# Memory attention by query rows, and a dilated layer whose keys and queries are made with tokens on the partitions

## The chip, the cores and the metric

The kernel runs on one core of a Trainium2 chip. The metric is device time in microseconds of one execution. TensorE (PE) multiplies, VectorE (DVE), ScalarE (ACT) and GpSimd (POOL) do the rest, SyncE (SP) issues the transfers. Engines run side by side, each through its own queue in order, and wait for each other through semaphores.

## What is computed

A network for 512 tokens of 1024 features: a first block (three kinds of attention, gates, a feed-forward part) and a second one (an mLSTM layer, a dilated-window layer, and a gated addition `ple` behind each). The two parts that the change touches:

```python
def memory_attention(cq, mk, mv):          # 4 heads of 128, 256 memory rows
    logits = jnp.einsum('bshd,bmhd->bhsm', cq, mk).astype(jnp.float32) * C_HEAD_DIM ** -0.5
    p = jax.nn.softmax(logits, axis=-1).astype(mv.dtype)
    return jnp.einsum('bhsm,bmhd->bshd', p, mv).reshape(bsz, seq, C_DIM)

def shared_kv(h, norm_g, w_kv, knorm_g, cos, sin):
    kv = (rms_norm(h, norm_g) @ w_kv).astype(jnp.float32)
    k, v = jnp.split(kv, 2, axis=-1)       # 4 heads of 128 each
    k = apply_rope(rms_norm(k, knorm_g), cos, sin)
    return k, v

def dilated_layer(h, k, v, norm_g, w_in, qnorm_g, w_out, cos, sin):
    proj = rms_norm(h, norm_g) @ w_in
    q, z = jnp.split(proj, [B_QW], axis=-1)            # 3 groups x 4 heads x 128, and 512
    q = apply_rope(rms_norm(q, qnorm_g), cos, sin)
    # group 0: window 128, step 1; group 1: window 512, step 4; group 2: window 2048, step 16
    # softmax of each group, the groups weighted by their log-denominators
    y = o.reshape(Bsz, S, B_VW) * jax.nn.silu(z.astype(jnp.float32))
    return y.astype(h.dtype) @ w_out
```

`rms_norm` is taken over the 1024 features of `h` (with gain `norm_kv` for K and V, `norm_b` for the rest) and again over the 128 features of each head of K and Q (gains `knorm`, `qnorm_b`).

## The kernel before

Activations lie feature-major: a tile of 128 features by 512 tokens, eight of them for 1024 features. A product in near-float32 is three fp32r matmuls of the operands' high and low halves (`mm3`: hi·hi, hi·lo, lo·hi). Weights come in units of 128 x 1024 float32 through SyncE's queue into `wraw` (two buffers); ScalarE rounds a unit to its high half `wh` (L154), and the low half `wl` is a subtraction on GpSimd (L158) or VectorE (L160), as the counter `pool_share` says (0.5: every second unit on GpSimd; 1.0: all; 0: none). A unit holds the eight 128 x 128 blocks of one output tile (24 matmuls of 512 columns), and a generator `fm_g` yields in the middle, so that "half a tile" is 12 matmuls. TensorE runs its instructions as they are coded; on the other engines a scheduler sets the order.

Memory attention (L655 to L715) weaves its steps with 20 half tiles of other products (queries of heads 2 and 3, and the gates): `logits(h)` makes memory rows by queries in two PSUM banks `zps`, copies them (L669), takes the maximum of both (L671) and over the partitions by an all-reduce on GpSimd (L673), subtracts it (L675) and takes the exponent; `values(h)` multiplies with `mv`, sums the columns by two matmuls with a matrix of ones (`colsum`), and divides through Ln and Exp, with `y` at L695. Behind it comes the stick-breaking attention, and the top-k search of the first attention runs on VectorE beside both.

The dilated layer makes each head's K and Q as a feature-major tile and calls `rope` on it: times the token's rms factor `bc` (L1370), squares in two halves `sqh`, `sql` (L1374 to L1376), the rotation (L1380 to L1383, two of its operations on GpSimd), and later, out of the list `todo`, the column sum over the head's 128 features, Ln, Exp and the product `q`, `kT`, `kTp` (L1391, L1394). 16 tiles go through it. The input's halves `xs` are split twice (`xsplit`, L241 and L242), once scaled by `norm_kv` and once by `norm_b`. `main` weaves `logits` and `values` of the four heads with the making of the other heads' Q and z; `logits(h)` ends with masks, a maximum, an all-reduce (L1500), subtractions and exponents; `values(h)` ends with `y` at L1539. Then `finish(h)` multiplies by silu(z) and splits, `out` and `prods` are the output product.

Of the kernel before, what the change touches and what calls it, by code (L numbers as in the profile page):

```python
# [47 lines left out]
def constants():  # L48
# [11 lines left out]
    cos, sin = np.cos(ang).T, np.sin(ang).T  # L60
    cos2 = np.concatenate([cos, cos], 0)
    sin2 = np.concatenate([sin, -sin], 0)
# [26 lines left out]
class K:  # L89
# [46 lines left out]
    def pre(s, *spec):  # L136
# [9 lines left out]
        if u == 0:  # L146
            for c in (slice(0, 512), slice(512, 1024)):
                s.split(hi[:, c], lo[:, c], raw[:, c])
            s.ready[spec] = hi, lo
            return  # L150
# [395 lines left out]
    def dsa_mem(s, x, iqc):  # L546
# [5 lines left out]
        with ExitStack() as br:  # L552
# [101 lines left out]
            with ExitStack() as c:  # L654
# [4 lines left out]
                zps = s.pool("zps", 2, PSUM, ctx=c)  # L659
# [4 lines left out]
                def logits(h):  # L664
                    z = wk.tile([128, 2, T], F32, name="z")
# [4 lines left out]
                    mx = s.tmp.tile([128, T], F32, name="t512")  # L670
                    nc.vector.tensor_tensor(mx, z[:, 0], z[:, 1], op=OP.max)  # L671
                    mb = wk.tile([128, T], F32, name="mb")
# [4 lines left out]
                    es = wk.tile([128, T], F32, name="es")  # L677
                    nc.gpsimd.tensor_tensor(es, z[:, 0], z[:, 1], op=OP.add)
                    e = [w1.tile([128, 2, T], F32R, name="e%d" % i) for i in range(2)]
                    s.split(e[0], e[1], z)  # L680
                    S = [w1.tile([128, T], F32R, name="S%d" % i) for i in range(2)]
                    s.split(S[0], S[1], es)
                    st[h] = e, S

                def values(h):
                    e, S = st.pop(h)
                    op = ops.tile([128, T], F32, name="ops")
                    for m in range(2):
                        s.mm3(op, [x[:, m, 128 * h:128 * h + 128] for x in mv], [x[:, m] for x in e], m == 0, m == 1)
                    dp = s.colsum(S[0], S[1], ops)  # L690
# [5 lines left out]
                    if s.dbg: s.dbg("attC%d" % h, y)  # L696
# [1002 lines left out]
```

## Time and profile before

| | |
|---|---|
| Time, median of 3 runs | 1631.87 us (1630.12 to 1631.94) |
| Profiled execution | 1637.18 us |
| Its span, first to last instruction | 1635.4 us |
| Granted TensorE clock, mean | 0.968 |
| Busy: PE, DVE, ACT, POOL | 1519.9, 1032.5, 704.3, 446.0 us |

The profile shows one execution. A busy share is the time in which an engine has an instruction in work; the matmuls' ends are modelled and overlap the next one's start, so their pace is read from starts. An idle time is put down to the instruction whose end released the engine.

### The profile page before, as it was taken

What the parts mean: (1) busy time and instruction counts of PE and PEld (TensorE: products, weight loads), DVE (VectorE), ACT (ScalarE), POOL (GpSimd) and SP (SyncE); (2) the same over time, 40 slices, a digit from 0 to 9 for tenths busy, and PEclk for the clock granted to TensorE, in tenths of its full rate; (3) what the DMA queues carried; (4) which work ended last, traced back from release to release, by engine and by line L of the source; (5) the groups of instructions that cost most, each with busy time, mean ns of one, the idle gap of its engine ahead of it and who ended that gap; (6) DMA issues with size and microseconds to landing.
All of it is one profiled execution on the core that took longest, in us unless ns stands there. A gap on an engine that the chain in (4) does not pass through costs nothing.

```text
span 1635.4 us, 17606 instructions
## 1 busy us (share of the span) xinstructions
PE 1519.9 (93%) x6717; PEld 1226.6 (75%) x6725; DVE 1032.5 (63%) x1313; ACT 704.3 (43%) x1019; POOL 446.0 (27%) x244
## 2 busy tenths in 40 slices
PE   8988998999999999999999998999999998867788
PEld 5866777777778887888888886778778786655677
DVE  7876878864766737433243337844576479878766
ACT  5633335454445545322232325343654365333553
POOL 3323432222311403110011105310120026865432
PEclk9998999999999999999999999999999999878999
DMA  5311322123222433332333333223212332311132
GB/s 192 115 52 52 93 76 77 52 65 103 84 80 82 136 116 127 98 103 91 99 95 100 94 97 122 78 78 117 65 52 78 132 108 64 102 52 39 39 123 97
DMA packets 44917, 148.11 MB, mean 91 GB/s; under 512 B 5280, under 2 KB 6688, under 8 KB 44576
## 3 DMA queue, kind: packets, MB, share of 16 engines
q1 hardware_dynamic: 44832, 146.98, 28.3%
q8 instruction: 53, 0.87, 0.2%
q14 instruction: 32, 0.26, 0.1%
HBM read 139.60 MB, written 6.29 MB: 89 GB/s over the span
## 4 chain that ended last, share of the span: by engine, by line
PE 56%; DVE 18%; ACT 7%; issue 6%; POOL 4%; DMA 2%; SPq 0%; POOLq 0%; DVEq 0%; ACTq 0%
PE dps L128 41%; PE b L128 10%; PE z L128 3%; POOL wl L158 1%; DVE e L808 1%; ACT e L122 1%; DVE e L809 1%; ACT t L122 1%; DVE sql L1376 1%; DVE t L1381 1%; PE aps L128 1%; DVE ss L290 1%; PE o L128 1%; DVE xl L242 1%; DVE t L1382 1%
## 5 line engine op out<-in xcount | busy, mean ns | idle before, releaser
L128 PE MATMUL dps<-xh,wl 128*128 128x512 f32 (+2 forms) x1092 | 430.3, 394 | 16.6 <-POOL wl L158 16.6
L128 PE MATMUL dps<-xh,wh 128*128 128x512 f32 (+2 forms) x1092 | 435.6, 399 | 7.0 <-DVE aTl L239 5.8
L128 PE MATMUL dps<-xl,wh 128*128 128x512 f32 (+2 forms) x1092 | 429.5, 393 | 4.5 <-DVE xl L242 4.5
L154 ACT ACTIVATE wh<-wraw 128x1024 fp32r<-128x1024 f32 x213 | 225.1, 1057 | 452.3 <-PE dps L128 280.6
L158 POOL TENSOR_TENSOR wl<-wraw,wh 128x1024 fp32r<-128x1024 f32 x88 | 224.0, 2546 | 535.3 <-ACT wh L154 351.5
L160 DVE TENSOR_TENSOR wl<-wraw,wh 128x1024 fp32r<-128x1024 f32 x151 | 191.2, 1267 | 170.1 <-ACT wh L154 169.5
L128 PEld LDWEIGHTS dps<-xh,wl 128*128 128x128 f32 (+1 forms) x1092 | 207.7, 190 | 62.3 <-POOL wl L158 17.8
L128 PEld LDWEIGHTS dps<-xh,wh 128*128 128x128 f32 (+1 forms) x1092 | 207.9, 190 | 57.4 <-DVE aTl L239 7.5
L128 PEld LDWEIGHTS dps<-xl,wh 128*128 128x128 f32 (+1 forms) x1092 | 207.8, 190 | 49.8 <-DVE xl L242 5.5
L1025 POOL TENSOR_TENSOR g<-g,bc 128x512 f32<-128x512 f32 x22 | 38.9, 1769 | 245.7 <-ACT g L122 245.7
L128 PE MATMUL b<-xl,wh 128*128 128x512 f32 x224 | 90.9, 406 | 8.1 <-DVE xl L242 8.0
L128 PE MATMUL b<-xh,wh 128*128 128x512 f32 x224 | 91.9, 410 | 3.0 <-ACT xh L241 1.6
L128 PE MATMUL b<-xh,wl 128*128 128x512 f32 x224 | 90.5, 404 | 4.0 <-DVE wl L160 3.9
L128 PE MATMUL dps<-fh,wh 128*128 128x512 f32 x176 | 69.3, 394 | 0.0
L128 PE MATMUL dps<-fh,wl 128*128 128x512 f32 x176 | 69.0, 392 | 0.0
L128 PE MATMUL dps<-fl,wh 128*128 128x512 f32 x176 | 68.3, 388 | 0.0
L128 PE MATMUL b<-wh,xh 128*128 128x512 f32 x160 | 63.5, 397 | 3.2 <-DVE y L695 2.2
L242 DVE SCALAR_TENSOR_TENSOR xl<-h,vecs,xh 128x512 fp32r<-128x512 f32 x56 | 60.3, 1092 | 6.8 <-ACT xh L241 6.7
L128 PE MATMUL b<-wl,xh 128*128 128x512 f32 x160 | 62.9, 393 | 0.8 <-DVE wl L160 0.8
L128 PE MATMUL b<-wh,xl 128*128 128x512 f32 x160 | 63.0, 394 | 0.0
L128 PEld LDWEIGHTS b<-xl,wh 128*128 128x128 f32 x224 | 43.5, 194 | 21.3 <-DVE xl L242 11.4
L1034 DVE TENSOR_TENSOR f<-dps,g 128x512 f32<-128x512 f32 x20 | 13.8, 692 | 67.3 <-PE dps L128 64.4
(366 smaller groups left out, 2676.9 us busy)
## 6 DMA issues: line engine op xcount, KB each, us to landing
wraw<-in_W SPq DMA_DIRECT2D x239, 512.0 KB, 3.6
h<-in_x SPq DMA_DIRECT2D x16, 256.0 KB, 4.0
pw<-pwo SPq DMA_DIRECT2D x16, 256.0 KB, 2.5
pw<-pw SPq DMA_DIRECT2D x2, 2048.0 KB, 7.8
strip<-in_relb SPq DMA_DIRECT2D x8, 256.0 KB, 2.7
out<-h SPq DMA_DIRECT2D x7, 256.0 KB, 2.0
G<-in_mem SPq DMA_DIRECT2D x1, 1024.0 KB, 9.0
praw<-in_p SPq DMA_DIRECT2D x2, 512.0 KB, 3.9
```

The lines of the kernel that those rows point to most:

```text
L122: i = s.nc.scalar.activation(out, in_, func, **kw)
L128: s.nc.tensor.matmul(out, l, r, start=start, stop=stop, skip_group_check=True)
L154: nc.scalar.activation(hi, raw, AF.Copy)
L158: nc.gpsimd.tensor_tensor(lo, raw, hi.bitcast(F32), op=OP.subtract)
L160: nc.vector.tensor_tensor(lo, raw, hi.bitcast(F32), op=OP.subtract)
L242: nc.vector.scalar_tensor_tensor(lo, src, scale, hi.bitcast(F32), op0=OP.mult, op1=OP.subtract)
L290: nc.vector.tensor_tensor(S[0], S[0], t, op=OP.add)
L808: nc.vector.tensor_tensor_scan(e[:, ::-1], keep, e[:, ::-1], 0.0, op0=OP.mult, op1=OP.add)
L809: nc.vector.tensor_tensor(c, c, e, op=OP.subtract)
L1025: nc.gpsimd.tensor_tensor(g, g, st["bc"], op=OP.mult)
L1376: nc.vector.tensor_tensor(sql, sq, sqh.bitcast(F32), op=OP.subtract)
L1381: nc.vector.tensor_tensor(t2[0:64], x[64:128], cs[64:128, T:], op=OP.mult)
```

## The change

Memory attention makes its logits the other way round: 128 query rows by 256 memory rows, four of them in the two banks `z`. The maximum and the sum are then along the row (a reduction on VectorE, an accumulator of ScalarE's exponent), the division is a multiply per row, and the result is transposed back by eight 128 x 128 transposes a head (`transp`) ahead of `values`. The all-reduce, the sum `es` and the column sums are gone.

The dilated layer makes K, Q (three groups of four tiles) and V in a new way, `quad`: the fixed side of the matmul is 128 tokens of `xs` (for K and Q every fourth token, so that a tile holds one class modulo 4), the moving side the weights of four tiles, 512 columns. `rope` then works on 128 tokens by four tiles: squares summed along the row by ScalarE's accumulator, the rotation wholly on VectorE, the factors as small 128 x 16 operations. `turned` transposes back to feature-major tiles, out of which `keys` and `queries` copy; they are called as hooks in the middle of the next group's product. The gains `norm_kv` and `norm_b` are multiplied into the weights as they are split (`quad` units in two pieces of 512 columns, `fmg` units in eight of 128), so that `xs` is split once, unscaled, where the `ple` before makes it; `knorm` and `qnorm_b` go into the tables of cosines by two multiplies at the start. `pool_share` is 0, and the additions of `logits` move to VectorE. The column sum in `values` becomes one float32 product with ones. The written order of the layer is new too; the host gives the tables with tokens on the partitions.

```diff
 def logits(h):                               # memory attention
-    for m in range(2):
-        zp = zps.tile([128, T], F32, name="zps")
-        s.mm3(zp, [k[:, h, 128 * m:128 * m + 128] for k in mk], cq[h], True, True)
-        nc.scalar.activation(z[:, m], zp, AF.Copy)
-    nc.vector.tensor_tensor(mx, z[:, 0], z[:, 1], op=OP.max)
-    nc.gpsimd.partition_all_reduce(mb, mx, 128, RMAX)
-    for m in range(2):
-        nc.vector.tensor_tensor(z[:, m], z[:, m], mb, op=OP.subtract)
-    s.act(z, z, AF.Exp, scale=sc)
-    nc.gpsimd.tensor_tensor(es, z[:, 0], z[:, 1], op=OP.add)
+    for t in range(4):
+        s.mm3(zt[:, t], [q[:, qt] for q in cq[h]], [k[:, h] for k in mk], t % 2 == 0, True)
+    nc.vector.tensor_reduce(mx, zt, mybir.AxisListType.X, OP.max)
+    nc.vector.tensor_scalar(nm, mx, -sc, None, op0=OP.mult)
+    for t in range(4):
+        s.act(e[:, t], zt[:, t], AF.Exp, scale=sc, bias=nm[:, t:t + 1], accum_out=sm[:, t:t + 1])
+    nc.vector.reciprocal(rs, sm)
+    for t in range(4):
+        nc.vector.tensor_scalar(e[:, t], e[:, t], rs[:, t:t + 1], None, op0=OP.mult)
 def main():
     for h in range(4):
         logits(h)
-        yield 4 if h else 3
+        yield 2 if h else 3
         if h:
+            transp(h - 1)
+            yield 2
             values(h - 1)
-    yield 4
+    yield 2
+    transp(3)
+    yield 2
     values(3)
     yield 1
...
+def quad(wname, c0s, gain, hooks, classes=True):
+    pss = [s.b4.tile([128, T], F32, name="b4") for _ in range(4)]
+    for k in range(8):
+        if k % 2 == 0:
+            u = s.w("quad", wname, tuple(c0s), k // 2, gain)
+        c = slice(512 * (k % 2), 512 * (k % 2) + 512)
+        for t in range(4):
+            r = slice(t, T, 4) if classes else slice(128 * t, 128 * t + 128)
+            s.mm3(pss[t], (xs[0][:, k, r], xs[1][:, k, r]), (u[0][:, c], u[1][:, c]), k == 0, k == 7)
+        for f in hooks.get(k, ()):
+            f()
+    return pss
...
+r = rstd_g()
+pk = quad("w_kv_2", [128 * h for h in range(4)], "norm_kv", {2: [lambda: next(r)], 4: [lambda: next(r)]})
+XK = rope(pk, ck)
+X0 = qquad(0, {5: [keys]})
+X1 = qquad(1, {5: [lambda: queries(X0, QS[0])]})
+logits(0)
+z_tile(0)
+pv = quad("w_kv_2", [512 + 128 * h for h in range(4)], "norm_kv", {5: [lambda: queries(X1, QS[1])]}, False)
...
+logits(1)
+z_tile(1)
+X2 = qquad(2, {4: [lambda: values(0)]})
+z_tile(2)
+values(1)
+z_tile(3)
+for h in range(2):
+    finish(h)
+queries(X2, QS[2])
+logits(2)
+out = s.fm4_g("w_out_b_2", [128 * m for m in range(4)], xs, ev, ks=range(4))
+prods(4, range(2))
+logits(3)
+next(out)
+next(out)
+values(2)
+finish(2)
+next(out)
+values(3)
+finish(3)
```

Where memory attention's head 2 begins, TensorE had before (`e`, `S` of the head before, `ops` a PSUM bank, `mk` and `cq` of head 2):

```order
L128 MATMUL ops<-e_964,mv_194 128x512
L128 MATMUL ops<-e_965,mv_194 128x512
L128 MATMUL ops<-e_964,mv_195 128x512
L128 MATMUL ops<-S_968,onesr 128x512
L128 MATMUL ops<-S_969,onesr 128x512
L128 MATMUL zps<-cq_934,mk_192 128x512
L128 MATMUL zps<-cq_935,mk_192 128x512
L128 MATMUL zps<-cq_934,mk_193 128x512
```

Of the change, the same engine at the transposes of head 1 (`ops<-csts,e`; the `dps` rows are the other products):

```order
L128 MATMUL dps<-xl,wh 128x512
L128 MATMUL dps<-xh,wl 128x512
L696 MATMUL ops<-csts,e 128x128 x8
L128 MATMUL dps<-xh,wh 128x512
L128 MATMUL dps<-xl,wh 128x512
```

Two half tiles later, the end of that head's values and the beginning of head 2's logits:

```order
L128 MATMUL dps<-e_1085,mv_194 128x512
L128 MATMUL dps<-e_1086,mv_194 128x512
L128 MATMUL dps<-e_1085,mv_195 128x512
L128 MATMUL z<-mk_192,cq_934 128x256
L128 MATMUL z<-mk_193,cq_934 128x256
L128 MATMUL z<-mk_192,cq_935 128x256
```

The column sums are gone, eight transposes stand two half tiles ahead of the values, and a matmul of the logits has half as many columns.

GpSimd in the middle of the dilated layer, before (`rx` rotated tiles, `mb` the all-reduce; a row that names no tile belongs to the one behind it):

```order
L158 TENSOR_TENSOR wl_10755<-wraw_10752,wh_10754 128x1024
L1516 TENSOR_TENSOR ws_10427<-ws_10427,l_10409 128x384
L1383 TENSOR_TENSOR rx_10571<-t512_10579,t512_10580 128x512
L1394 TENSOR_TENSOR q1_10518<-rx_10517,t512_10588 128x512
L1500 ISA
L1500 ISA mb_10609<-mx_10605 128x512
L158 ISA
L158 TENSOR_TENSOR wl_10841<-wraw_10838,wh_10840 128x1024
L1380 TENSOR_TENSOR t512_10665<-rx_10657,late_9711 128x512
```

The last rows that GpSimd has in that layer after the change, and the next two of its queue:

```order
L1537 ISA
L1537 ISA mb_10497<-mx_10493 128x512
L1537 ISA mb_10761<-mx_10757 128x512
L1537 ISA mb_11225<-mx_11221 128x512
L1537 ISA mb_11273<-mx_11269 128x512
L166 ISA
L166 TENSOR_TENSOR wl_11518<-wraw_11515,wh_11517 128x1024
L166 TENSOR_TENSOR wl_11548<-wraw_11545,wh_11547 128x1024
```

The four all-reduces follow each other with nothing between them, and the `wl` rows behind them belong to the `ple` after the layer.

VectorE near the layer's end, before (`l_11000` are head 3's logits, `mb` the all-reduce of their maximum, `y32` head 2's result up to its gate at L1559 and its low half `xl` at L239):

```order
L1503 TENSOR_TENSOR l_11000<-l_11000,mb_11008 128x4x128
L1504 TENSOR_TENSOR l_11000<-l_11000,mb_11008 128x3x128
L1506 TENSOR_TENSOR l_11000<-l_11000,mb_11008 128x4x128 x2
L1535 TENSOR_TENSOR t512_11094<-dps_11081,t512_11094 128x512
L1539 TENSOR_TENSOR y32_9718<-t512_11094,t512_11097 128x512
L253 TENSOR_TENSOR zs_9717<-dps_11068,bc_9830 128x512
L1559 TENSOR_TENSOR y32_9718<-y32_9718,zs_9717 128x512
L160 TENSOR_TENSOR wl_11200<-wraw_11197,wh_11199 128x1024
L1514 TENSOR_TENSOR ws_11018<-a23_11016,l_11000 128x512
L239 TENSOR_TENSOR xl_98<-y32_9718,xh_97 128x512
```

VectorE at the same place after the change (`l_11251` head 3's logits; L1575 is head 2's `y`, L1578 its gate, L247 its low half, kept in the buffer `kT`):

```order
L1553 TENSOR_TENSOR ws_11235<-ws_11235,l_11203 128x384
L1571 TENSOR_TENSOR t512_11332<-dps_11320,t512_11332 128x512
L1540 TENSOR_TENSOR l_11251<-l_11251,mb_11273 128x4x128
L1541 TENSOR_TENSOR l_11251<-l_11251,mb_11273 128x3x128
L1543 TENSOR_TENSOR l_11251<-l_11251,mb_11273 128x4x128 x2
L1575 TENSOR_TENSOR kT_9754<-t512_11332,t512_11335 128x512
L1578 TENSOR_TENSOR kT_9754<-kT_9754,zs_9758 128x512
L1548 TENSOR_TENSOR a23_11281<-l_11251 128x512
L1551 TENSOR_TENSOR ws_11283<-a23_11281,l_11251 128x512
L247 TENSOR_TENSOR xl_98<-kT_9754,xh_97 128x512
```

Head 3's subtractions stand ahead of head 2's `y` in both; the low half of a weight unit and a z tile's product between them are gone, and two sums of weights stand there.

## Rows read from the trace of the kernel before

**Rows 1.** Windows: busy us of PE, PEld, DVE, ACT, POOL; clock, DMA, GB/s.

```profile
87.00:181.00 94.00, 75.61 (x299) 60.24 (x297) 67.58 (x148) 33.75 (x47) 28.99 (x21) 0.89 0.19 62
181.00:490.00 309.00, 292.67 (x1362) 235.09 (x1368) 227.89 (x324) 141.67 (x208) 90.24 (x41) 0.98 0.25 76
490.00:1333.00 843.00, 822.70 (x3601) 668.25 (x3603) 439.31 (x529) 345.46 (x497) 140.72 (x82) 0.99 0.31 98
1333.00:1584.00 251.00, 205.38 (x853) 164.57 (x851) 189.72 (x180) 111.02 (x158) 142.51 (x76) 0.90 0.23 72
```

**Rows 2.** TensorE's waits, 87 to 182 us: total us, times, longest.

```profile
PE dps L128 <- POOL wl L158: 16.6, 3, 9.7
PE b L128 <- DVE y L695: 2.2, 1, 2.2
```

**Rows 3.** Timeline of GpSimd, 130 to 146 us.

```profile
133.66 1.85 POOL L673 PARTITION_ALL_REDUCE mb<-t  x1 [7.10 <-DVE score L728]
142.44 2.83 POOL L158 TENSOR_TENSOR wl<-wraw,wh 128x1024 fp32r<-128x1024 f32 x1 [6.93 <-issue]
```

**Rows 4.** Timeline of TensorE, 1425 to 1452 us: 24 matmuls from one to the other.

```profile
1434.75 0.39 PE L128 MATMUL dps<-xh,wh 128*128 128x512 f32 x1
...
1440.19 0.40 PE L128 MATMUL aps<-sqh,onesr 128*128 128x512 f32 x1
```

**Rows 5.** TensorE's waits, 1333 to 1584 us.

```profile
PE aps L128 <- ACT t L122: 17.1, 5, 7.9
PE aps L128 <- DVE sql L1376: 12.5, 4, 4.7
PE dps L128 <- DVE xl L242: 4.5, 2, 2.9
```

**Rows 6.** VectorE by lines and shapes, 1333 to 1584 us: count, busy us, mean ns.

```profile
L1376 DVE TENSOR_TENSOR sql<-t,sqh 128x512 fp32r<-128x512 f32 x16 | 24.2, 1515 | 0.6 <-ACT sqh L1375 0.2
```

**Rows 7.** Timeline of VectorE, 1433 to 1443 us: head 1's maximum and subtractions.

```profile
1432.66 1.21 DVE L1491 SCALAR_TENSOR_TENSOR l<-z,late 128x1024 f32<-128x1024 f32 x1
1433.90 1.12 DVE L1495 TENSOR_TENSOR mx<-l 128x512 f32<-128x512 f32 x1
1435.05 0.69 DVE L1497 TENSOR_TENSOR mx<-mx,l 128x512 f32<-128x512 f32 x1
1435.78 0.56 DVE L1498 TENSOR_TENSOR mx<-mx,l 128x384 f32<-128x384 f32 x1
...
1441.71 0.69 DVE L1503 TENSOR_TENSOR l<-l,mb 128x512 f32<-128x512 f32 x1 [2.62 <-POOL mb L1500]
...
1442.78 1.09 DVE L1506 TENSOR_TENSOR l<-l,mb 128x512 f32<-128x512 f32 x1
```

**Rows 8.** Timeline of TensorE, 125 to 130 us.

```profile
126.41 0.63 PE L128 MATMUL dps<-xl,wh 128*128 128x512 f32 x1
126.83 0.63 PE L128 MATMUL dps<-xh,wl 128*128 128x512 f32 x1
```

**Rows 9.** Timeline of TensorE, 243 to 248 us: transposes.

```profile
244.94 0.82 PE L739 MATMUL dps<-csts,e 128*128 128x128 f32 x6
245.59 0.60 PE L739 MATMUL aps<-csts,e 128*128 128x128 f32 x4
```

**Rows 10.** ScalarE by lines and shapes, whole span: exponent with accumulator.

```profile
L122 ACT ACTIVATION_READ_ACCUMULATOR l<-l,sx 128x1 f32 x32 | 6.0, 186 | 0.0
L122 ACT ACTIVATE l<-l,sx 128x128 f32<-128x128 f32 x8 | 3.2, 402 | 22.1 <-DVE sx L930 22.1
```

**Rows 11.** TensorE by lines and shapes, whole span: float32 product with ones.

```profile
L128 PE MATMUL aps<-ss,csts 128*128 128x512 f32 x10 | 6.0, 686 | 1.8 <-DVE ss L290 1.8
```

**Rows 12.** ScalarE by lines and shapes, whole span: copies out of PSUM.

```profile
L669 ACT ACTIVATE z<-zps 128x512 f32<-128x512 f32 x8 | 4.5, 591 | 0.0
L1533 ACT ACTIVATE t<-dps 128x512 f32<-128x512 f32 x4 | 4.3, 1082 | 5.4 <-PE dps L128 5.4
```

**Rows 13.** Weight loads by lines and shapes, 1333 to 1584 us.

```profile
L128 PEld LDWEIGHTS dps<-xh,wh 128*128 128x128 f32 x140 | 27.0, 193 | 7.2 <-ACT t L1533 1.4
```

More of the change, by code (lines that the diff above doesn't have):

```diff
@@ L148, in pre @@
                 s.split(hi[:, c], lo[:, c], raw[:, c])
+            s.ready[spec] = hi, lo
+            return
+        if spec[0] in ("quad", "fmg"):
+            n = 2 if spec[0] == "quad" else 8
+            for i in range(n):
+                c = slice(1024 // n * i, 1024 // n * (i + 1))
+                s.split(hi[:, c], lo[:, c], raw[:, c], s.vec(spec[-1], spec[3] * n + i))
             s.ready[spec] = hi, lo
@@ L680, in logits @@
[L680 to L683, printed above, removed]
+                    zt = zpp.tile([128, 4, 256], F32, name="z")
+                    for t in range(4):
+                        qt = slice(128 * t, 128 * t + 128)
+                        s.mm3(zt[:, t], [q[:, qt] for q in cq[h]], [k[:, h] for k in mk], t % 2 == 0, True)
+                    sx = wk.tile([128, 16], F32, name="sx")
@@ L1459, in fill @@
-            def fill():
-                for h in range(1, 4):
-                    for g in range(3):
-                        yield from q_g(h, g)
-                for m in range(4):
-                    yield from z_g(m)
-            for g in range(3):
-                s.drain(q_g(0, g))
-            zpp = s.pool("zps", 1, PSUM, ctx=ph)
+            q3 = s.pool("dq", 3, ctx=ph)
+            xp = s.pool("dx", 5, ctx=ph)
+            s.b4 = s.pool("b4", 4, PSUM, ctx=ph)
+            rg = s.tmp.tile([128, T], F32, name="t512")
@@ new lines, in turned, with keys @@
+            def turned(X, j):
+                ps = s.dps.tile([128, T], F32, name="dps")
+                for c in range(4):
+                    nc.tensor.transpose(ps[:, 128 * c:128 * c + 128], X[c][:, j], s.cst("ident"))
+                return ps
+            def keys():
+                for h in range(4):
+                    ps = turned(XK, h)
+                    nc.scalar.activation(kTp[:, h], ps, AF.Copy)
+                    nc.vector.tensor_copy(kT[:, h].rearrange("p (a c) -> p c a", c=4),
+                                          ps.rearrange("p (c a) -> p c a", c=4))
@@ new lines, in dilated, with queries @@
+            qt = {}
+            def queries(X, tiles):
+                for j, (h, g) in enumerate(tiles):
+                    if g == 0:
+                        qt[h] = q3.tile([128, T], F32, name="q1"), q3.tile([128, 4, 2, 128], F32, name="q23")
+                    ps = turned(X, j).rearrange("p (c a) -> p c a", c=4)
+                    if g == 0:
+                        nc.vector.tensor_copy(qt[h][0].rearrange("p (a c) -> p c a", c=4), ps)
+                    else:
+                        nc.scalar.activation(qt[h][1][:, :, g - 1, :], ps, AF.Copy)
@@ L1539, in values @@
                 nc.vector.tensor_tensor(y32[:, h], t, rd, op=OP.mult)
-            def main():
-                yield 4
-                for h in range(4):
-                    logits(h)
-                    yield 3
-                    if h:
-                        values(h - 1)
-                    if h < 3:
-                        yield 3
-                yield 99
-                for h in range(3):
-                    finish(h)
-                next(out)
-                next(out)
-                next(out)
-                values(3)
             def finish(h):
@@ L1564, in ev @@
                 s.ssq_add(s.S, s.h[:, m])
-            out = s.fm4_g("w_out_b_2", [128 * m for m in range(4)], xs, ev, ks=range(4), banks=lambda: zpp.tile(
-                [128, 4 * T], F32, name="z"))
-            s.weave(main(), fill())
-            s.pool_share = 0.0
             us, pss = {}, {}
```

258 lines of the change are left out of this document (131 added, 127 removed).

## Prediction

> **What bounds the kernel now.** I read the windows first [rows 1]. TensorE carries the kernel: in the two long stretches 181 to 490 and 490 to 1333 us it is busy for 293 of 309 and 823 of 843 us, and its granted clock is 0.98 and 0.99. The change touches neither. The two stretches that it rewrites are the two loose ones: memory attention (87 to 181, TensorE 75.6 of 94.0 us, clock 0.89) and the dilated layer (1333 to 1584, 205.4 of 251.0 us, clock 0.90). No other engine fills either of them, so the question is what TensorE waits for there.
>
> The list of waits says it. In memory attention, [rows 2]: 16.6 us in three waits for `wl` of line 158, the low half of a weight unit that GpSimd makes, and 2.2 us for `y` at the end. GpSimd's own timeline has the reason [rows 3]: the all-reduce of line 673 is a record of 1.85 us, but GpSimd shows nothing for 7.1 us ahead of it and 6.9 us behind it, and the `wl` that stands next in its queue starts only at 142.44. An all-reduce takes GpSimd out for some 15 us, in which TensorE uses nearly three units (a unit is 24 matmuls, 5.44 us in [rows 4], 0.227 each).
>
> In the dilated layer the waits come to 45.6 us over eight lines; [rows 5] has the three largest, 34.1. 29.6 of it is the `aps` column sum: the exponent, or the square's low half `sql`, is late. VectorE is slow while GpSimd works, which it does there for 142.5 of 251 us: `sql` takes 1515 ns on average [rows 6], where VectorE operations of the same size take 690 in a stretch in which GpSimd has only its all-reduce [rows 7].
>
> [...] In the memory stretch 299 matmuls by 0.227 are 67.9 us, waits 18.8, so about 7 us are the slower level. In the dilated one the work is 713 products of 512 columns (161.9 us), the logits (about 20) and at most 16 us of small ones by their records: 198 us, waits 45.6, so some 7 are left there too.
>
> **The change, memory attention.** The same 20 half tiles of other products lie between the steps: 240 matmuls by 0.227 are 54.5 us. The heads' own: 24 value matmuls, 5.4 us, stay; 24 logits matmuls of 512 columns become 48 of 256, half as long each, 5.5 us as before; the eight column sums go (1.8 us); 32 transposes come. Six transposes in a row took 0.82 us and the four behind start 0.65 us after the first [rows 9]: 0.11 us each, 3.5 us. Sum 69.
>
> The chain of a head is now a row maximum on VectorE over 1024 columns, four exponents with their sums on ScalarE (for 128 columns 402 + 186 ns each [rows 10]), a reciprocal, four multiplies: about 6 us, and its transposes come after two to four half tiles more (2.7 us each) and another head's logits. The transposed halves have two half tiles, 5.4 us, for a copy (0.6) and a subtraction (0.7) each, twice. Both fit. GpSimd has only every second `wl` left there, 2.8 us [rows 3] of each 10.9, so nothing is late. What covers all this is the 54.5 us of other products; if VectorE's queue is long, each of the four heads can lose one or two microseconds. I take 3 us of stalls (bounds 0 and 8), slower level included: 72 us for 94. **Gain 22.** Of it I take 2 back, because VectorE, busy for 67.6 us of this stretch before, has to put the same top-k work into less time, and the next stretch waits for it at its start.
>
> **The change, dilated layer.** TensorE: 40 column-sum matmuls go (9.1 us); 64 transposes come (7.0); the four sums of weights become single products in full float32, each two instructions of 686 ns [rows 11], 5.5 us; the eight small statistics 0.5. Work: +4 us, so 202. The 45.6 us of waits go with what they waited for: no column sum, no `sql`, no scaled second split of the input (`xl` of line 242, 4.5 us), no `q` on GpSimd. GpSimd keeps four all-reduces and nothing else.
>
> What comes in their place, by the written order:
> - VectorE and ScalarE per group of four tiles, against 96 matmuls, 21.8 us. ScalarE: four copies out of PSUM (0.59 [rows 12]), sixteen squares with sums (0.59 by [rows 10]), eight scaled halves of weights (0.7), about 19 with two turned tiles. VectorE: eight halves and four times five operations of the rotation at 0.7 [rows 7], the 64-column parts less, about 20. Both are below 21.8, not by much: I put nothing, and 5 us for each of three groups if one of them runs over (a rival).
> - Keys: turned inside the next group, after 16 us; the fourth turned tile waits for VectorE's strided copy of the second, which stands behind weight halves: 2 us.
> - Statistics at the start 0.8; queries of the first two groups 1.3 together.
> - Queries of the third group: no further group covers the rotation, only two z tiles (10.9 us), `values(1)` and `finish`: 3 us.
> - The end. Head 3's four subtractions stand on VectorE ahead of head 2's `y`, and wait for the all-reduce. From the end of logits(3), by [rows 7]: masks 2.8 (1.21 for 1024 columns, 1920 in five pieces), maxima 2.4, a weight half of 1024 columns 1.2, the all-reduce 5.3 (the last maximum ends at 1436.3, the subtraction that needs it starts at 1441.7), subtractions 3.4, `y`, its gate and the low half 2.1, a hand-over or two: 18.5. TensorE has two rounds of the output product (5.5) and `values(2)` (4.1) meanwhile. It waits 8.5 us.
> - Rest 1. **Sum of waits 16.6, for 45.6.**
>
> Transfers: the sixteen small `vq` transfers stay on SyncE's queue and now hold up the units of the third group by some 10 us; the unit buffers that are ahead and the z tile cover that, and I put nothing.
>
> Weights are now the moving side and tokens the fixed one, every fourth token for 384 of the 672 products. TensorE's load record is 193 ns for contiguous columns [rows 13], under a matmul's 227 and beside it. Nothing here shows a load of every fourth element. Nearest rows: a ScalarE copy that writes in that step takes 1082 ns where a plain one takes 591 [rows 12], a VectorE maximum 1.12 against 0.69 us [rows 7]: 0.8 to 0.96 ns more per element, which puts 0.11 us on a load of 128. Loads start as close as 0.11 us (the transposes of [rows 9] have one each), so 0.11 + 0.11 would still lie under 0.227. Bounds: 0, and a fourfold floor, 0.44 us. I take 4 us, near the lower end, because the row that the load is nearest to is its own, beside a matmul.
>
> Slower level: fewer and shorter gaps, 2 us for 7. So 45.6 - 16.6 - 4 - 4 + 5 = **26 us gained**: 225 for 251.
>
> Sum: 22 - 2 + 26 = 46. The profiled run was 1637.2 us; less 46 is 1591. It stood 5.3 above the median 1631.9; by that median the forecast is **1586 us**. Within 0.2% (3.3 us) of the median no measurement of this kernel can tell a change from none.
>
> **Rivals.**
> - *Strided loads bound.* For it: both strided rows above cost more. Against it: the load lies beside the matmul. It costs when a load passes 0.227 us. At 0.30 it is 384 x 0.073 = 28 us, 24 more than taken: 1610. The sign turns at 0.227 + 50/384 = 0.357; at 0.44 it is 82 us: 1664, slower. [...]
> - *VectorE or ScalarE becomes the bound of the groups.* For it: 19 and 20 of 21.8 us, in-order queues, PSUM buffers that are freed by them. If each of the three groups loses 5 us more: 1601. Against it: uncontended durations are at hand once GpSimd is idle.
> - *Memory's gain is given back.* For it: VectorE has 67.6 of 94 us of work there, now against 72. If the stick-breaking part waits for top-k: 10 to 15 us back, 1598.
> - *The waits go wholly.* Scheduling hides the end and the keys: 1572.
>
> **How the numbers follow.** Forecast (1572 to 1598, mechanisms as said): 0.58. VectorE or ScalarE, or memory given back (1598 to 1612): 0.22. Loads cost 20 to 46 us (1602 to 1628): 0.07. They just cancel the gain: 0.03. They cost over 53 us, slower: 0.07. Better than 1572: 0.03. The range that leaves out 2 in 10: 1570 to 1612. Faster 0.90, same 0.03, slower 0.07.
>
> **What would show it.** Right: the memory stretch 70 to 75 us with no `wl` wait; the dilated one 220 to 230; no DVE operation of that layer over 1.3 us that is not strided; the largest wait of TensorE there is for `xl` near the end, 6 to 10 us; matmuls in the groups start 0.227 apart. Wrong: matmuls of the class groups start further apart than those of the V group, whose tokens are contiguous (strided loads); or gaps at each `b4` bank (evacuation late); or new gaps at the first stick-breaking product.

## The result, and the profile after

The changed kernel takes 1579.88 us, the median of 4 runs (1577.55 to 1580.14), against 1631.78 for the kernel before (4 runs): ratio 0.9681 (95% interval 0.9664 to 0.9698), 52 us less. Forecast was 1586, 46 less. The profiled execution took 1579.89 us, with a span of 1578.1.

The windows of the profile after, in the stages of [rows 1] (PE, PEld, DVE, ACT, POOL; clock, DMA share, GB/s):

```profile
86.60:161.80 75.20, 71.61 (x346) 59.65 (x345) 72.51 (x166) 29.76 (x63) 16.34 (x13) 0.98 0.24 76
161.80:470.00 308.20, 292.42 (x1367) 234.54 (x1372) 226.98 (x320) 138.76 (x203) 90.12 (x41) 0.98 0.25 77
470.00:1312.20 842.20, 823.50 (x3596) 665.62 (x3597) 439.85 (x531) 345.23 (x498) 137.45 (x81) 0.99 0.31 98
1312.20:1524.90 212.70, 200.31 (x894) 179.89 (x894) 155.12 (x272) 109.13 (x292) 10.53 (x5) 0.97 0.26 85
```

From the first matmul of memory attention's logits to the first of the stick-breaking part it is now 75.2 us (94.3 before), and from the dilated layer's first matmul to the first one of the `ple` behind it 212.6 us (251.3). The 1151.2 us between them became 1150.4, the end grew by 1.7. Together with 0.6 at the start that is 57.3 us of span; the profiled execution before stood 5.4 us above its median, and the first experiment shows where such a difference lies.

TensorE's waits in memory attention after (total, times, longest), to be read against [rows 2]:

```profile
PE dps L128 <- DVE e L247: 3.0, 1, 3.0
PE dps L128 <- ACT e L246: 0.6, 1, 0.6
```

No wait for a `wl` is left; 3.6 us wait for the halves of head 2's transposed weights. And the five longest of the dilated layer, against [rows 5]:

```profile
PE b L128 <- ACT xh L246: 4.7, 1, 4.7
PE dps L1470 <- DVE kT L1477: 1.9, 1, 1.9
PE dps L128 <- DVE a L1548: 1.8, 1, 1.8
PE aps L128 <- DVE ws L1553: 1.2, 1, 1.2
PE b L128 <- DVE xl L247: 0.9, 1, 0.9
```

All of them together are 12.4 us, where it was 45.6. Four of the five (`xh`, `a`, `ws`, `xl`, 8.6 us in all) are the end of the layer, where head 2 is late: `a` and `ws` ahead of its values, `xh` and `xl` behind its result.

### The profile page after: what moved, and what is told of

It reads as the page before. It is cut to its first block, busy times and chain, and to the rows that moved or that the text cites. A ratio compares the mean times of both kernels' runs of the same rounds, so it can differ in the third digit from the quotient of the medians.

```text
span 1578.1 us, 17864 instructions
## 1 busy us (share of the span) xinstructions
PE 1513.0 (96%) x6805; PEld 1238.7 (78%) x6813; DVE 1004.1 (64%) x1421; ACT 696.4 (44%) x1168; POOL 301.9 (19%) x165
## 4 chain that ended last, share of the span: by engine, by line
PE 70%; DVE 18%; ACT 7%; issue 3%; POOL 1%; DMA 1%; SPq 0%; DVEq 0%; ACTq 0%; POOLq 0%
PE dps L128 46%; PE b L128 18%; PE z L128 3%; DVE ss L298 2%; DVE xl L250 1%; DVE e L821 1%; PE aps L128 1%; ACT e L122 1%; DVE wl L168 1%; DVE e L822 1%; ACT wh L162 1%; PE o L128 1%; DVE score L741 1%; DVE aTl L247 1%; DVE e L687 1%
## 5 line engine op out<-in xcount | busy, mean ns | idle before, releaser
L128 PE MATMUL dps<-xh,wh 128*128 128x512 f32 (+2 forms) x996 | 396.4, 398 | 6.0 <-DVE aTl L247 5.8
L128 PE MATMUL dps<-xl,wh 128*128 128x512 f32 (+2 forms) x996 | 388.4, 390 | 0.0
L128 PE MATMUL dps<-xh,wl 128*128 128x512 f32 (+2 forms) x996 | 388.1, 390 | 0.0
L166 POOL TENSOR_TENSOR wl<-wraw,wh 128x1024 fp32r<-128x1024 f32 x66 | 164.8, 2498 | 454.6 <-ACT wh L162 298.3
L128 PE MATMUL b<-wh,xh 128*128 128x512 f32 x288 | 115.8, 402 | 0.0
L128 PE MATMUL b<-wl,xh 128*128 128x512 f32 x288 | 114.6, 398 | 0.0
L128 PE MATMUL b<-wh,xl 128*128 128x512 f32 x288 | 114.3, 397 | 0.0
L128 PEld LDWEIGHTS b<-wh,xh 128*128 128x128 f32 x288 | 70.0, 243 | 7.1 <-issue 0.2
L128 PEld LDWEIGHTS b<-wl,xh 128*128 128x128 f32 x288 | 70.1, 243 | 6.7
L128 PEld LDWEIGHTS b<-wh,xl 128*128 128x128 f32 x288 | 70.0, 243 | 6.7
```

The costliest lines, as they stand in the source:

```text
L128: s.nc.tensor.matmul(out, l, r, start=start, stop=stop, skip_group_check=True)
L166: nc.gpsimd.tensor_tensor(lo, raw, hi.bitcast(F32), op=OP.subtract)
```

## Experiments

Each experiment's ratio is to runs of the kernel before from its own series (medians 1629.9 for the first to fourth experiment, 1630.6 for the fifth to eighth, 1632.2 for the rest). Stretches are those of the section above.

**1. The kernel before once more.** No edit.

> The kernel before once more, unchanged, for a second profile. By the two traces the span fell by 57.3 us, by the medians the time fell by 51.9: the profiled execution of before stood 5.4 us above its median. Theory: that execution was long by chance, in the dilated layer, where waits are longest; a second profile shows a span near 1630 and a dilated stretch of 246 us instead of 251, all other stretches within 1 us. Rival: every profiled execution of it is long, and the span is 1635 again.

One execution of 1623.58 us, profiled. Windows, the untouched stretch and the dilated layer:

```profile
180.90:1321.70 1140.80, 1107.14 (x4961) 897.16 (x4970) 666.83 (x851) 487.77 (x706) 231.45 (x123) 0.99 0.29 93
1321.70:1570.20 248.50, 206.14 (x853) 164.95 (x852) 193.65 (x180) 111.16 (x158) 142.03 (x76) 0.90 0.23 73
```

Neither was right. The dilated stretch is 248.5 us, 2.7 less, but the untouched stretch is 1140.8 us instead of 1151.2. Counted from the starts of its matmuls in both traces, some 6 of these 10.4 us are matmuls at the lower clock level (0.50 in the records, where the other is 1.00; 86 of them start 0.37 to 0.46 us apart in the first profile, 57 in this one) and some 3 are longer gaps. In the fourteen profiles of this study that stretch, the same 4960 matmuls in all of them, takes 1140.8 to 1151.5 us. So a few us of the time belong to no edit, and stretches are the better measure here: memory attention took 93.8 to 94.3 us in four profiles of its old form and 75.2 in eight of nine of its new one (76.4 in the other).

**2. Memory attention alone.** The kernel before, with `logits`, `transp`, `values` and `main` of the change.

> The kernel before with the new memory attention alone. Theory: the two parts are independent; the memory stretch falls from 94 to 75 us as in the whole change, no wait for wl of GpSimd is left in it, and the time is 1612 to 1614 us. Rival: half of what memory attention gains is taken back later by the top-k search on VectorE, and only the whole change hides that: 1620.

1608.79 us (1605.72 to 1614.52), ratio 0.9866 (0.9831 to 0.9900). The stretch is 75.2 us, with the same 3.6 us of waits; the layer behind keeps 247.8. The gain is the part's own, 19.0 us, and nothing of it is given back: the time fell by 21 us (16 to 28), and with the whole change the 309.0 us behind it [rows 1] took 308.2.

**3. The dilated layer alone.** The change, with memory attention of before.

> The change without its memory attention, which is that of before. Theory of independent parts: the dilated stretch takes 212 to 214 us as in the whole change, memory attention 94, and the time is 1596 to 1600 us. Rival, that the parts help each other: above 1603.

1599.18 us (1598.67 to 1600.41), ratio 0.9802 (0.9772 to 0.9831). Memory attention 94.1, the dilated stretch 212.1. The parts are independent: 19.0 and 39 us by stretches, and by time 21.1 and 30.7, together the change's 52. Of the layer's 39 us the time shows 31; 1.7 are lost behind the layer and some 5 ahead of it (experiment 9).

**4. Tokens in a row as the fixed side.**

```diff
-                        r = slice(t, T, 4) if classes else slice(128 * t, 128 * t + 128)
+                        r = slice(128 * t, 128 * t + 128)
```

> The changed kernel in which the groups of K and Q take 128 tokens in a row as their fixed side instead of every fourth token; the rest treats them as classes, so that its keys and queries belong to other tokens than the reference's. Theory: the step of 16 bytes makes a load 0.31 us instead of 0.19 and lengthens the pace of 384 matmuls from 0.2267 to 0.2367 us; without it the pace is 0.2267 and the time 3.8 us less than the changed kernel, 1576. Rival 1: the slower pace of these groups comes from something else (the b4 banks, ScalarE and VectorE reading at the same time), and 1580 and 0.2367 stay. Rival 2: loads with a step also delay what stands behind them, and more than 8 us are gained, under 1572.

1574.99 us (1574.55 to 1576.20); the dilated stretch 208.1 instead of 212.6. Matmuls of the third group of queries start 0.2267 us apart, 0.2350 in the change. Weight loads by lines and shapes (count, busy us, mean ns), the changed kernel first, where 128 of the 160 loads of `xh` have the step and 32, those of V, have not:

```profile
L128 PEld LDWEIGHTS b<-wh,xh 128*128 128x128 f32 x160 | 46.0, 288 | 2.1 <-issue 0.2
L128 PEld LDWEIGHTS dps<-xl,wh 128*128 128x128 f32 x44 | 8.3, 188 | 2.1 <-issue 0.5
```

The same row with tokens in a row:

```profile
L128 PEld LDWEIGHTS b<-wh,xh 128*128 128x128 f32 x160 | 30.4, 190 | 6.5 <-issue 0.2
```

The step makes a load longer by some 0.12 us (128 loads of 0.31 and 32 of 0.19 give the mean of 288 ns), but since it lies beside a matmul only 0.008 to 0.010 us of it come out for each of 384: 3 to 4 us, where 4 had been taken.

**5. GpSimd emptied, with the old layout.** The kernel before; `pool_share` 0 in the dilated layer, and of its GpSimd operations only the all-reduces stay:

```diff
-                nc.gpsimd.tensor_tensor(t1, x, cs[:, :T], op=OP.mult)
+                nc.vector.tensor_tensor(t1, x, cs[:, :T], op=OP.mult)
-                nc.gpsimd.tensor_tensor(x, t1, t2, op=OP.add)
+                nc.vector.tensor_tensor(x, t1, t2, op=OP.add)
-                        nc.gpsimd.tensor_tensor(dst, x, r, op=OP.mult)
+                        nc.vector.tensor_tensor(dst, x, r, op=OP.mult)
```

> The kernel before, with its own feature-major dilated layer, but with everything except the four all-reduces taken from GpSimd there and given to VectorE: the low halves of the weights, three operations of each rotation, two additions of each head. Theory: the gain of the dilated part needs the new layout, since the chain of each tile (two squares, low half, column sum, Ln, Exp, product) and its VectorE work stay; VectorE's operations get short (0.69 instead of 1.1 to 2.8 us), but it has 28 halves of weights and 48 operations more, about 70 us, and becomes the bound: 245 to 255 us for the stretch, 1627 to 1637 in all. Rival: the assignment to GpSimd alone was the fault; the waits for the column sum fall to under 10 us, the stretch to 220 to 230 and the time to 1605 or less.

1592.26 us (1591.54 to 1595.21), ratio 0.9769 (0.9744 to 0.9793): the rival, and more than it asked. The window of the layer, TensorE's two longest waits in it, and two rows of VectorE's operations:

```profile
1327.20:1538.90 211.70, 196.97 (x854) 160.40 (x852) 184.09 (x248) 111.00 (x158) 13.24 (x7) 0.96 0.27 85
```

```profile
PE aps L128 <- DVE sql L1376: 6.5, 4, 1.9
PE aps L128 <- ACT t L122: 6.0, 4, 2.3
```

```profile
L160 DVE TENSOR_TENSOR wl<-wraw,wh 128x1024 fp32r<-128x1024 f32 x26 | 32.3, 1242 | 6.7 <-ACT wh L154 6.5
L1376 DVE TENSOR_TENSOR sql<-t,sqh 128x512 fp32r<-128x512 f32 x16 | 10.9, 685 | 0.1
```

The stretch is 211.7 us, as with the new layout (212.1 and 212.6), though the 32 column-sum matmuls, `sql` and both splits of the input are all there. `sql` takes 685 ns, 1515 in [rows 6]. VectorE was given 21 low halves (26 in the row, 5 before) and 48 operations more, and is busy for 184 us, less than the 189.7 of [rows 1]: what it was given is what its own operations no longer lose. The time fell by 38 us, more than with the new layout alone (31, experiment 3).

**6. Low halves off GpSimd in memory attention.** The kernel before, with one line:

```diff
             s.mark("mem")
+            s.pool_share = 0.0
             yh, yl = s.ynew()
```

> The kernel before, with its own memory attention and its all-reduces, but with the low halves of the weights on VectorE in that stretch. Theory: of the 19 us the 16.6 us of waits and most of the slower clock come from the low halves that stand behind an all-reduce in GpSimd's queue; taking them off the queue alone gives 12 to 19 us, 1613 to 1620. Rival: the all-reduce's length is itself what TensorE waits for, or VectorE has no room for ten more halves (12 us): within 4 us of before.

1621.57 us (1619.61 to 1625.17), ratio 0.9944 (0.9927 to 0.9961). The stretch falls from 94.3 to 80.5 us, 13.8 of the 19.0. TensorE's waits there:

```profile
PE b L128 <- DVE y L696: 8.5, 1, 8.5
PE ops L128 <- ACT t L122: 2.6, 1, 2.6
```

No `wl` any more; the end waits 8.5 us for the last head's `y`, whose all-reduce, exponent, Ln and Exp follow one another. The query rows bring 5.2 us more: these waits, 11.7 us with a third one of 0.6, become 3.6, for some 2 us of work more on TensorE. The time fell by 9.0 us only (6 to 12). Part of the rest is lost just behind: TensorE comes out of the 8.5 us at its lower level (clock 0.91 over the next 30 us, 1.00 there in experiment 2). What remains is within what the untouched stretch varies by.

**7. Another order at the end.** The changed kernel; the fourth z tile goes behind logits(3), which needs the result's halves in buffers of their own:

```diff
+            values(0)
+            X2 = qquad(2, {})
             z_tile(1)
-            X2 = qquad(2, {4: [lambda: values(0)]})
-            z_tile(2)
             values(1)
-            z_tile(3)
+            z_tile(2)
...
             logits(3)
+            z_tile(3)
             next(out)
```

> The changed kernel with another written order at the end of the dilated layer: values(0) before the third group of queries, the z tiles one place later each, the fourth z tile behind logits(3); the result's halves go to buffers of their own so that xs stays whole for that tile (the table of K shares a buffer with the logits, and the queries have two buffers instead of three). Theory: the 8.6 us that TensorE waits for head 2 (a, ws, xl) and some 2 us of slower clock fall to 2 to 3 us; 1571 to 1574. Rival: the queries of the third group are then late instead, since less work lies behind that group: within 2 us of 1580, or slower.

Slower: 1590.95 us (1589.01 to 1593.45), ratio 0.9756 (0.9731 to 0.9781), the stretch 220.7. TensorE's three longest waits:

```profile
PE b L128 <- ACT ys L246: 4.8, 1, 4.8
PE dps L128 <- DMA vq<-v: 4.0, 2, 3.8
PE b L128 <- ACT xh L249: 2.0, 1, 2.0
```

`values(0)` now comes before the sixteen small transfers of `vq` have landed (4.0 us). The wait for `xh` is the first matmul of the `ple` behind the layer. At the end `ys` still waits 4.8 us. The windows of the end say why, the changed kernel's 28 us first, then this one's 30:

```profile
1476.00:1504.00 28.00, 20.06 (x97) 15.81 (x95) 27.39 (x40) 12.17 (x17) 3.86 (x2) 0.96 0.11 38
```

```profile
1482.00:1512.00 30.00, 24.69 (x109) 19.99 (x108) 28.28 (x41) 12.47 (x17) 4.39 (x2) 0.90 0.18 53
```

VectorE is busy for 27.4 of 28 us and 28.3 of 30. Other work on TensorE didn't hide a queue that is full here; the z tile has even put two operations more into it. The order of TensorE was not what held the end.

**8. Half of the rotation back on GpSimd.** The changed kernel:

```diff
-                    nc.vector.tensor_tensor(
+                    nc.gpsimd.tensor_tensor(
                         t1.rearrange("p (j f) -> p j f", j=4), x,
...
-                    nc.vector.tensor_tensor(x.rearrange("p j f -> p (j f)"), t1, t2, op=OP.add)
+                    nc.gpsimd.tensor_tensor(x.rearrange("p j f -> p (j f)"), t1, t2, op=OP.add)
```

> The changed kernel with two of the five full-width operations of its rotation (the product with the cosines and the final addition) on GpSimd, 32 operations of 512 columns. Theory: while GpSimd works, VectorE's two-input operations beside it take 1.1 us or more instead of 0.69, and the rotation's end moves past the place where the next group turns its tiles: 8 to 20 us lost, 1588 to 1600. Rival: the groups hide it and VectorE is relieved by 22 us: no change or faster, 1576 to 1581.

1590.38 us (1589.53 to 1591.15), ratio 0.9754 (0.9730 to 0.9777); the stretch 223.9, 11.3 more. VectorE's half products (L1452) and an operation after the rotation (L1463), in the changed kernel:

```profile
L1452 DVE TENSOR_TENSOR t<-rx,late 128x256 f32<-128x256 f32 x24 | 9.0, 418 | 0.0
L1463 DVE TENSOR_TENSOR rx<-rx,rf 128x512 f32<-128x512 f32 x16 | 10.0, 683 | 0.1
```

and here:

```profile
L1452 DVE TENSOR_TENSOR t<-rx,late 128x256 f32<-128x256 f32 x24 | 26.1, 1140 | 6.0 <-ACT rx L1437 6.0
L1463 DVE TENSOR_TENSOR rx<-rx,rf 128x512 f32<-128x512 f32 x16 | 10.1, 685 | 0.1
```

The operations that now run beside GpSimd go from 418 to 1140 ns, those that don't stay at 685. VectorE, relieved of 32 operations, is busy for 167 us in place of 155. TensorE waits 19.3 us, where it was 12.4, and the clock over the layer is 0.94 instead of 0.97.

**9. The old layout with one sum.** Fifth experiment's layer with the new memory attention, and

```diff
-                sq = s.tmp.tile([128, T], F32, name="t512")
-                sqh = pool.tile([128, T], F32R, name="sqh")
-                sql = pool.tile([128, T], F32R, name="sql")
+                sq = pool.tile([128, T], F32, name="sqh")
                 nc.scalar.activation(sq, x, AF.Square)
-                nc.scalar.activation(sqh, x, AF.Square)
-                nc.vector.tensor_tensor(sql, sq, sqh.bitcast(F32), op=OP.subtract)
...
-                    a = s.colsum(sqh, sql)
+                    a = s.aps.tile([128, T], F32, name="aps")
+                    s.mm(a, s.cst("ones"), sq, True, True)
```

> The new memory attention with the feature-major dilated layer of before, GpSimd emptied there as in the fifth run, and its column sums made as one full float32 product of the squares with ones (no split of the squares: one square and one subtraction less for each of the 16 tiles; the same for the sum of the weights). Theory: what made the dilated layer faster is an idle GpSimd, not the token layout; with the chain in front of the column sum shorter by two operations the 12.5 us of waits for it fall to 3 to 6, the stretch from 211.7 to 200 to 206 us, and the time is 1567 to 1575, below the changed kernel. Rival: the full float32 product or the deferred part (Ln, Exp, product) sets the wait, and the stretch stays at 210 to 213, 1577 to 1582.

1565.57 us (1563.28 to 1566.89), ratio 0.9593 (0.9572 to 0.9613): below both kernels. The layer's window and TensorE's waits in it:

```profile
1306.30:1512.30 206.00, 198.38 (x853) 156.39 (x852) 172.90 (x228) 100.45 (x138) 12.66 (x7) 0.99 0.27 88
```

```profile
PE b L128 <- DVE kT L1375: 2.5, 2, 1.8
PE aps L128 <- ACT t L122: 2.2, 2, 1.5
PE z L128 <- DVE q L1393: 1.8, 1, 1.8
PE z L128 <- DVE xl L239: 1.0, 1, 1.0
```

206.0 us with 7.5 us of waits, at a clock of 0.99: 6.6 us less than the changed kernel's layer. The float32 sums themselves are dearer for TensorE than the pairs that they replace, as one of them shows:

```profile
1345.12 1.02 PE L128 MATMUL aps<-sqh,csts 128*128 128x512 f32 x2
1345.58 0.79 PE L128 MATMUL b<-wh,xh 128*128 128x512 f32 x1
1346.20 0.39 PE L128 MATMUL b<-wl,xh 128*128 128x512 f32 x1
```

From 1345.12 to 1346.20 lie the sum's two instructions and one product of 0.227 us, so the sum takes 0.85 us where two fp32r matmuls take 0.45: some 8 us for twenty sums, which shorter waits and a better clock more than pay back. The next start behind a float32 product is recorded 0.03 us after it; only the one after that shows the price.

Another 7 us lie in the untouched stretch (1143.6 here, 1150.4 there). Five of them have a pattern: over all distances of 0.20 to 0.26 us between matmul starts there (some 4230 in each profile) the mean is 0.2290 to 0.2291 us in each of the eight profiles of kernels with the token layout and 0.2278 to 0.2279 in each of the six with the old one: 0.0012 by 4230 are 5 us. TensorE's code there is the same (at its end VectorE and ScalarE also split `xs` in the kernels with the token layout). It isn't spread evenly: the 528 matmuls of the feed-forward product (`dps<-fh,wh` and its two companions) start 0.2290 us apart in each of the six and 0.2333 in each of the eight, the 2350 or so of `dps<-xh,wh` and its companions 0.2275 and 0.2276. Why is not shown.

**10 and 11. Steps of two and of eight.** The changed kernel with the fixed side of the K and Q groups taken so:

```diff
-                        r = slice(t, T, 4) if classes else slice(128 * t, 128 * t + 128)
+                        o = 256 * (t // 2) + t % 2
+                        r = slice(o, o + 255, 2) if classes else slice(128 * t, 128 * t + 128)
```

(step eight: every eighth element of two feature blocks, 1017 elements).

> The changed kernel whose groups of K and Q take every second of 256 tokens as their fixed side (8 bytes between elements); its keys and queries belong to other tokens than the reference's. [...] Rival, that the load slows with the step or with any step: 0.22 to 0.32 us.

> The changed kernel whose groups of K and Q take every eighth element of two feature blocks in a row as their fixed side (32 bytes between elements); its keys and queries mix features and are not the reference's. [...] Rival, cost that grows with the step: 0.4 us or more, and the pace 0.3 or more, 30 us slower than the changed kernel.

One execution each: 1578.04 and 1583.09 us. Loads at step two, then at step eight, 128 of 160 with the step:

```profile
L128 PEld LDWEIGHTS b<-wh,xh 128*128 128x128 f32 x160 | 31.4, 196 | 6.7 <-issue 0.2
```

```profile
L128 PEld LDWEIGHTS b<-wh,xh 128*128 128x128 f32 x160 | 48.2, 301 | 2.1 <-issue 0.2
```

With 32 plain loads of 190 ns taken out the loads take 0.197 us at step two, 0.312 at four, 0.329 at eight. Matmuls of the third group start 0.2333, 0.2350 and 0.2445 us apart, 0.2267 without a step. So the load itself jumps between two and four and hardly grows behind, and the rival of a growing cost falls; but the pace is a little slower at step two already, and slower again at eight with a load hardly longer; why is not shown.

**12. GpSimd's subtractions between the all-reduces.**

```diff
             queries(X2, QS[2])
+            s.pool_share = 1.0
             logits(2)
```

> The changed kernel with the low halves of the output product's weights on GpSimd from logits(2) on, so that its queue again has subtractions between the all-reduces of heads 2 and 3. Theory: GpSimd's 7 us of nothing before and behind an all-reduce in the kernel before belong to the change from one kind of instruction to the other, since in the changed kernel an all-reduce takes under 2 us from the maximum to the subtraction; with subtractions between them the 7 us come back, head 2's and 3's subtractions are late and the time grows by 8 to 20 us, 1588 to 1600. Rival: VectorE, busy for 27.4 of the 28 us in which the tail waits, is relieved of three halves of 1.2 us, and the time falls by 2 to 4 us.

1589.30 us (1586.50 to 1589.94), ratio 0.9741 (0.9718 to 0.9764), 9 us slower. GpSimd's timeline at the end, in the changed kernel, where an all-reduce begins 0.2 us after its maximum (1486.0):

```profile
1486.16 1.78 POOL L1537 PARTITION_ALL_REDUCE mb<-mx  x1 [49.95 <-DVE mx L1535]
1494.67 2.08 POOL L1537 PARTITION_ALL_REDUCE mb<-mx  x1 [6.72 <-DVE mx L1535]
```

and here, with TensorE's longest wait below it:

```profile
1485.95 1.81 POOL L1537 PARTITION_ALL_REDUCE mb<-mx  x1 [8.14 <-DVE mx L1535]
1494.80 2.48 POOL L166 TENSOR_TENSOR wl<-wraw,wh 128x1024 fp32r<-128x1024 f32 x1 [7.05 <-DVE a L1548]
1503.77 1.80 POOL L1537 PARTITION_ALL_REDUCE mb<-mx  x1 [6.49 <-issue]
```

```profile
PE b L128 <- ACT xh L246: 10.7, 1, 10.7
```

The first all-reduce is the same. Between it and the `wl` lie 7.05 us (the profile names an addition of VectorE there, which ended 0.8 us before the `wl`; the 6.93 us of [rows 3] end with nothing that it shows), and the next all-reduce, whose maximum is ready at 1493.3, begins at 1503.77. The 7 us in [rows 3] are not the all-reduce's but the change from one kind of instruction to another.

## Why the prediction was right, and which steps were not

**Memory attention: right in cause and size.** 72 us forecast, 75.2 measured. Of the 3.2 us, 0.6 are waits (3.6 in all, 3 taken with the slower level), 1.7 the clock (3.4 us at the lower level) and 0.9 the work. The 2 us that I took back for the top-k search were not lost (experiment 2). The cause was put too coarsely: the all-reduce (1.85 us in [rows 3]) doesn't take GpSimd out, the change of kind does, twice (7.05 and 6.49 us in experiment 12); what GpSimd does in that time no row shows. Experiment 6 splits the gain of the stretch: 13.8 us come from taking `wl` out of that queue, 5.2 from the query rows.

**Dilated layer: right in sign, too small, and wrong in the reason.** I had 26 us, it was 38.6. By the sum's terms:
- Waits after: 16.6 forecast, 12.4 measured. The keys' 2 stood (1.9); the third group's queries, 3 us, waited for nothing. The 8.5 at the end came out as 8.6 partly by luck: by their own terms they are 8.9 (18.5 - 5.5 - 4.1), and where I had them, behind head 2's result, TensorE waits 5.6 us; the other 3.0 are head 2's sums `a` and `ws`, which were not in the sum.
- The logits, "about 20", and the slower level, "some 7". This term failed. Of the old kernel's logits I had read the pace, about 5 us for a head, in places where TensorE ran at its lower level. Windows around a head's sixteen matmuls, in the kernel before and then in the changed one; the clock is the number behind the five engines:

```profile
1460.30:1465.80 5.50, 5.50 (x16) 4.50 (x15) 5.12 (x5) 2.36 (x4) 3.63 (x3) 0.54 0.00 0
```

```profile
1478.30:1481.30 3.00, 3.00 (x17) 2.69 (x16) 3.00 (x7) 2.07 (x5) 0.00 (x0) 1.00 0.45 160
```

At full rate fourteen of them start 0.216 us apart and two 0.108: 3.25 us a head, 13 for four. Some 7 us that I held for work were clock, or (2.3 us in head 3) a wait that the 45.6 already count. Work of the old layer at full rate: 162 + 13 + 16 of small ones = 191; 251.3 - 191 - 45.6 leaves 15 for the slower level, not 7. The 7 us were what the other terms left and the 2 us after the change my estimate; no row shows either. What the clock's records show is 0.50 from 125 to 130 us in the kernel before, behind TensorE's wait of 9.7 us, and 1.00 from 131 us. They agree with the 15: 47.8 us of the layer are at the lower level, 17.6 of them waits, and of the other 30 half is lost. In the changed layer 13.7 us are at the lower level, 2.2 of them waits: 6 lost. So the clock gave 9 us where I had 5.
- Work added, +4, and the step of sixteen bytes, 4: together 8 forecast, 4 measured, as what is left of 38.6 after 33.2 of waits and 9.4 of clock. The step is 3 to 4 of them (experiment 4). The four float32 sums were priced too high: 686 ns is the record of an instruction that overlaps the next, and a sum takes 0.85 us (experiment 9), 3.4 us for four heads and not 5.5.
- Sum: 33 (waits) + 9 (clock) - 4 (work and steps) = 38.

That the whole came within 6 us of 1586 is luck in part: the layer gave 12.6 us more than forecast, and some 7 of them were lost ahead of it and behind it, where the forecast had nothing.

**The reason.** "The 45.6 us of waits go with what they waited for: no column sum, no `sql`" was the step that failed as a cause. Experiment 5 keeps both and the waits fall to 14.8 us all the same. I had seen that VectorE is slow while GpSimd works, and still priced GpSimd's emptying as a by-product; before that experiment I expected VectorE to become the bound. What makes the old layer as fast as the new one is that GpSimd's elementwise work is taken away: `sql`, 0.68 to 2.78 us before (1515 ns on average), takes 685 ns, and the chain in front of each column sum gets shorter. Experiment 8 puts a part of that work back, into the new layout, and loses 11.3 us. The trace of before shows two ways in which that work delays TensorE. VectorE's own operation is slow beside it: `sql` takes 0.69 us while GpSimd shows nothing and 1.64 us later on. And the chain stands in GpSimd's queue: ScalarE's Ln, which freed TensorE after its longest wait (7.9 us), had itself waited for the end of a rotation there, behind an all-reduce and the 7 us that follow it.

```profile
1438.39 0.69 DVE L1376 TENSOR_TENSOR sql<-t,sqh 128x512 fp32r<-128x512 f32 x1
1458.00 1.64 DVE L1376 TENSOR_TENSOR sql<-t,sqh 128x512 fp32r<-128x512 f32 x1
```

```profile
1439.87 1.80 POOL L1500 PARTITION_ALL_REDUCE mb<-mx  x1 [5.80 <-ACT t L122]
1448.65 1.25 POOL L1380 TENSOR_TENSOR t<-rx,late 128x512 f32<-128x512 f32 x1 [6.97 <-issue]
1452.17 1.25 POOL L1383 TENSOR_TENSOR rx<-t,t 128x512 f32<-128x512 f32 x1
```

```profile
1453.46 0.69 ACT L122 ACTIVATE t<-aps,epsc 128x512 f32<-128x512 f32 x1 [5.57 <-POOL rx L1383]
```

Experiments 5 and 8 move both at once, so how the 38 us divide between the two is not shown. That the token layout itself is worth anything is not shown: it brings 212.1 us where the old one brings 211.7, with a shorter chain the old one does 206.0, and the layout goes with 5 us more in the stretch ahead (experiment 9). Why VectorE's operations are slow beside GpSimd's (1515 against 685 ns in experiment 5, 1140 against 418 in experiment 8) is not shown.

**The rivals.** *Strided loads bound* fell: the load is longer, as the row of ScalarE's strided write had said (0.12 us for 128 elements), but at 0.31 us, past the 0.227 from which I had let it cost its whole excess, it still stays beside the matmul. The 28 us that I had for a load of 0.30 came out as 3 to 4, 0.008 to 0.010 us for each of 384 (experiment 4). *VectorE becomes the bound* came true in one place, the end of the layer (27.4 of 28 us), not in the groups. *Memory's gain is given back* fell.

**What would have shown it.** Memory at 75.2 without a `wl` wait: no such wait, and 0.2 above the range. The dilated stretch below 220: outside. The largest wait: at the end, but for `xh` and 4.7 us, where 6 to 10 for `xl` had been named. The class groups against the V group, 0.235 to 0.237 against 0.227: the sign that I had named for strided loads, at 3 to 4 us and not 28.

## What to carry to other kernels

Read the price of an operation only where TensorE's granted clock is 1.00, not from records that overlap but from starts, and up to the second start behind it, since the first can be recorded too early (0.03 us behind a float32 product, where a sum takes 0.85, experiment 9). When VectorE's operations of one shape take anything between 0.7 and 2.8 us, as `sql` did here, first take the elementwise work off GpSimd and give VectorE the whole of it, one line at a time, before a layout is rewritten; here that line of edits alone gave what the rewrite gave (38 us of time against 31). Keep instructions of one kind together in GpSimd's queue: a change took 7.05 and 6.49 us in experiment 12, and an all-reduce behind another began 0.2 us after its maximum.

## What was unexpected of the hardware

GpSimd took about 7 us between an all-reduce and a subtraction, in either direction (7.05 and, from the subtraction's end at 1497.28, 6.49 us in experiment 12), and none between the all-reduces of the changed kernel's end: 0.2 us after the maximum the next one began. A fixed side with 8 bytes between its elements loaded nearly as fast as one in a row (0.197 against 0.190 us), and its matmuls still started 0.007 us further apart; why is open. The same 4960 matmuls took 1140.8 to 1151.5 us from one profiled execution to another, and they start 0.0012 us further apart on average (0.0044 in the feed-forward product) in every kernel that has the token layout later on.
